# Weight sums issued by GpSimd in 45 marked steps of up to eight DMAs

## The chip, the cores and the metric

The kernel runs on one core of a Trainium2 chip. A core has TensorE (PE, matrix products), VectorE (DVE, elementwise), ScalarE (ACT, functions and copies), GpSimd (POOL) and SyncE (SP). SP, ACT and GpSimd also issue DMAs; each of the three has a queue of its own, and all share 16 DMA engines. The metric is the time of one execution on the device in microseconds. Three runs of the kernel before took 2488.29, 2488.68 and 2490.72 us.

## The reference

One decoder layer over 2048 tokens of width 1024, in float32, and a final norm:

```python
h = rmsnorm(x, mix_norm_g[l])
q, k, v, g, u = jnp.split(h @ w_in[l], [R, 2*R, 3*R, 4*R], axis=-1)      # R = 512
y_ret  = silu(g) * head_rmsnorm(retention(q, k, v, positions), ret_gn_g[l])   # 4 heads
y_pool = pool_mixer(u, pool_w[l], pool_scale[l])       # trailing means 2/4/8/16
x = x + jnp.concatenate([y_ret, y_pool], axis=-1) @ w_out[l]
x = x + cross_attn(rmsnorm(x, xa_norm_g[l]), mem_n, xa_wq[l], xa_wkv[l], xa_wo[l])   # 256 memory tokens
x = x + conv_glu_ffn(rmsnorm(x, ffn_norm_g[l]), ...)   # 2 x 2816 columns, causal conv of width 3
...
return rmsnorm(x, final_norm_g)
```

## The kernel before

Everything is kept transposed: a tile has 128 channels on the partitions and 512 tokens along the free side. Each float32 product is made from three matmuls in the reduced format fp32r (lines 266 to 268, the helper `passes`): high part by high part, high by low, low by high. A helper `split` (L258, ScalarE's copy, and L242, DVE's subtraction) makes the two parts.

The tokens go in two blocks of 1024 (`b` = 0 and 1). Block 0 passes through values, four retention heads, the pooling groups, the output projection (`add_residual`, whose x-tiles `fetch_x` loads at L556), the attention, and a projection with the folded value weights VWd. The attention multiplies with a folded score matrix Md: `load_m` (L905) fetches it in eight loads of 512 KB through the raw buffers R and S, and ScalarE splits each before its buffer is loaded again. At its first tile the attention also needs the norm of the tokens: squares on ScalarE (L387), sums on DVE (L242), and tiny matmuls (`stats`, L347) that add over the channels. Between the last tiles of block 0's attention DVE builds the rotary tables for block 1, which begins with a load of the positions (L585). During the VWd projection the tokens of block 1 are loaded and squared. Then block 1 runs: `values`, with `quarter_sums` (loads at L1524, ScalarE at L1532) beside it and the norm of the block (`stats`, a reciprocal root on DVE, and matmuls at L371 that spread it), then `head_projections`, output projection, attention and VWd projection. The feed-forward part of both blocks follows (`run`), from about 1225 us to the end.

In block 1's heads and in the whole feed-forward part a product of two by two blocks is made with seven block products instead of eight. That needs sums of blocks of the weights. They are made in DRAM by DMA: `weight_sums` (L975 to L994) is a generator over 42 jobs (8 of the input weights into Ad, 22 of w_up into Ud, 12 of w_dn into Dd). A job writes four blocks of 128 x 512 numbers (256 KB; 192 KB for four of the jobs) in five steps: SP copies two blocks (L986); GpSimd adds to both by accumulating DMAs (L988, L989); then twice a copy from a finished block (L992) and an addition to it (L994). Members of the feed-forward part and of block 1's heads load the finished sums later (L1070), through seven buffers of half a raw tile in block 1's heads.

The generator hangs in `under[0]`. The code that builds the matmuls takes one turn of it, `next(under[0], None)`, every so often: every second group of 12 matmuls in block 0's heads and pooling groups (`slow`), every group in the output projections, three turns per tile in block 0's attention and two in block 1's (`4 - pace`), one per call of `between` in block 1's values, one per product in block 1's heads. In the VWd projections it is set aside (`paused`). A turn places instructions in the program text only. The order on each engine is then chosen by a planner that simulates the kernel: instructions go by program order where they are ready, and later ones may run ahead. A job's copies on SP are bound only to come after the latest fetch on SP (`tc.issue_after(fetched[0].ins)`, order on that queue alone); GpSimd's DMAs wait for their data, and for nothing else. GpSimd has no other work in this part.

Of the kernel before, what the change touches and what calls it, by code (L numbers as in the profile page):

```python
# [11 lines left out]
AF = mybir.ActivationFunctionType  # L12
ALU = mybir.AluOpType
AX = mybir.AxisListType

P = 128
# [120 lines left out]
def trunk(ctx, tc, xT, memT, pos, w_qkgu, w_v, wkv, wqT, wo, wout_r, wout_p, poolT, w_up, w_dn, vecs, consts, outT):  # L137
# [162 lines left out]
        return X[:, 2 * k, s * SUB : (s + 1) * SUB], X[:, 2 * k + 1, s * SUB : (s + 1) * SUB]  # L300


    quarter, slow = [0], [True]
    behind, under, fetched = [iter(())], [iter(())], [None]
    turned, chained = [], []
    latest = [None]
# [585 lines left out]
    def attention(sums, beside, pace):  # L892
# [39 lines left out]
        for i in range(2 * KT):  # L932
# [20 lines left out]
            if len(late) == 2:  # L953
                turn(*late.pop(0))
            late.append((prob[hp], t, e))
            for _ in range(4 - pace):
                next(under[0], None)
            if i < KT - 2:
                next(more_m, None)
# [15 lines left out]
    def weight_sums():  # L975

        jobs = [((w_qkgu[a], w_qkgu[c]), 0, 4, Ad[p]) for p, (a, c) in enumerate(PAIRS)]
        jobs += [((w_up[f], w_up[f + NF]), 0, 4, Ud[f]) for f in range(NF)]
        for at, (k0, n) in enumerate(ROUNDS):
            jobs += [((w_dn[2 * j], w_dn[2 * j + 1]), k0, n, Dd[at, j]) for j in range(KT // 2)]  # L980
        for w, k0, n, to, in jobs:
            a11, a12, a21, a22 = (block(w, i // 2, i % 2, k0, n) for i in range(4))
            d = [to[i][:, : n * P] for i in range(4)]
            with tc.issue_after(fetched[0].ins):
                for i, a in ((2, a21), (0, a11)):
                    sp.dma_start(d[i], a)  # L986
            yield
            pool.dma_start(d[2], a22, accum_op=ALU.add, max_dma_last_dim=2048)  # L988
            pool.dma_start(d[0], a21, accum_op=ALU.add, max_dma_last_dim=2048)  # L989
            for at, was, a in ((1, 2, a11), (3, 1, a12)):  # L990
                yield
                pool.dma_start(d[at], d[was], max_dma_last_dim=2048)  # L992
                yield
                pool.dma_start(d[at], a, accum_op=ALU.add, max_dma_last_dim=2048)  # L994

    class Round:

# [861 lines left out]
    for b in range(NB):  # L1859
# [37 lines left out]
            mix = head_projections(b, v, rb, tabs, t1, t2, z3, z4)  # L1897
        for r in rb:
            r.free()
        slow[0] = False  # L1900

        xs = [TT.take() for _ in range(NS)]
        ahead = fetch_x(b, 0)
# [32 lines left out]
        def tables():  # L1936
            for got in rope_tables(b + 1):
                yield
            for i, r in enumerate(got):
                sp.dma_start(rope_d[i], r.f[:, :SUB])  # L1940
                r.free()

        beside = tables() if b + 1 < NB else first_tiles(own)
        prob, behind[0] = attention(xs, beside, b + 1)
        for _ in beside:
            pass
        under, paused = [iter(())], under
# [194 lines left out]
```

## Time and profile before

| What | us |
|---|---|
| median of three runs | 2488.68 |
| the profiled execution | 2485.41 |
| its span, first to last instruction | 2483.6 |
| PE busy | 2421.9 |
| DVE busy | 1728.7 |
| ACT busy | 1285.2 |
| POOL busy | 254.7 |

A wait in the profile is the idle time of an engine before an instruction, put down to what released it last. A DMA row gives the instruction's tiles (written <- read), the queue, the count, the size and the median time from issue to landing. In windows, the times are counted from the start of the span; the granted clock is 1.00 when TensorE runs at full speed.

### The profile page before, as it was taken

To read this page: it belongs to the slowest core of one execution; us is meant where nothing else is said; L and a number is where in the kernel's file an instruction comes from. 1 tells how busy PE (TensorE), PEld (TensorE's weight loads), DVE (VectorE), ACT (ScalarE), POOL (GpSimd) and SP (SyncE) were. 2 spreads that over 40 slices of the span, in tenths; PEclk is the share of its full clock that TensorE was granted. 3 is DMA by queue.
4 is the path that set the end of the run, shared out by engine and by line. 5 is a ranking of instruction groups with operands and counts; after the bars stand their busy time and mean duration, and the time that the engine had idled before them with its cause. 6 is when DMAs were issued, how large, how long until landed. Compare 5 with 4: busy or idle time off the path is not lost.

```text
span 2483.6 us, 33188 instructions
## 1 busy us (share of the span) xinstructions
PE 2421.9 (98%) x11294; PEld 2018.5 (81%) x11294; DVE 1728.7 (70%) x2921; ACT 1285.2 (52%) x2303; POOL 254.7 (10%) x356
## 2 busy tenths in 40 slices
PE   6999999899999999999999999999999999999997
PEld 6888888777777787888888888888888888888886
DVE  8646566555676666575688776897667688867875
ACT  6333423334444453434555555675555677666763
POOL 1110101352102222000000000020000000000000
PEclk9999999999999999999999999999999999999998
DMA  8463847998738779557458655665446468758951
GB/s 310 100 162 119 230 106 218 303 263 245 216 115 195 168 180 269 172 178 255 153 186 278 212 187 168 210 222 170 161 158 216 132 225 302 245 189 281 345 167 68
DMA packets 269820, 501.56 MB, mean 202 GB/s; under 512 B 28881, under 2 KB 58705, under 8 KB 269649
## 3 DMA queue, kind: packets, MB, share of 16 engines
q1 hardware_dynamic: 214352, 406.61, 49.0%
q0 software_dynamic: 30784, 64.50, 13.2%
q10 hardware_dynamic: 24512, 28.32, 3.3%
q8 instruction: 89, 1.46, 0.2%
q14 instruction: 83, 0.67, 0.1%
HBM read 398.13 MB, written 187.17 MB: 236 GB/s over the span
## 4 chain that ended last, share of the span: by engine, by line
PE 86%; DMA 6%; DVE 4%; ACT 2%; issue 1%; SPq 0%; POOLq 0%; POOL 0%; DVEq 0%; ACTq 0%
PE mm L266 27%; PE mm L268 27%; PE mm L267 27%; DMA T<-xT 2%; DMA Ud<-w_up 1%; DVE T L242 1%; DMA T<-pos 1%; DMA T<-Xd 1%; DVE Z L242 1%; PE aux L266 1%; PE aux L771 1%; PE aux L782 1%; PE aux L267 1%; PE aux L798 1%; PE aux L268 1%
## 5 line engine op out<-in xcount | busy, mean ns | idle before, releaser
L266 PE MATMUL mm<-G,Q 128*128 128x512 f32 (+1 forms) x1745 | 672.4, 386 | 22.1 <-ACT Q L258 11.7
L268 PE MATMUL mm<-G,Q 128*128 128x512 f32 (+1 forms) x1745 | 669.1, 384 | 5.9 <-DVE Q L242 5.7
L267 PE MATMUL mm<-G,Q 128*128 128x512 f32 (+1 forms) x1617 | 619.5, 383 | 0.0
L267 PE MATMUL mm<-G,E 128*128 128x512 f32 x1084 | 421.6, 389 | 0.0
L266 PE MATMUL mm<-G,E 128*128 128x512 f32 x1084 | 420.0, 389 | 0.0
L268 PE MATMUL mm<-G,E 128*128 128x512 f32 x1084 | 419.2, 389 | 0.0
L266 PEld LDWEIGHTS mm<-G,Q 128*128 128x128 f32 x1745 | 331.0, 190 | 88.8 <-ACT Q L258 13.3
L268 PEld LDWEIGHTS mm<-G,Q 128*128 128x128 f32 x1745 | 330.3, 189 | 71.4 <-DVE Q L242 8.7
L267 PEld LDWEIGHTS mm<-G,Q 128*128 128x128 f32 x1617 | 306.8, 190 | 56.2
L242 DVE TENSOR_TENSOR Z<-Z,mm 128x512 f32<-128x512 f32 x296 | 201.3, 681 | 98.5 <-PE mm L268 98.3
L250 DVE SCALAR_TENSOR_TENSOR Z<-Z,vecs 128x1024 f32<-128x1024 f32 x176 | 224.5, 1279 | 50.0 <-ACT Z L1139 46.4
L268 PEld LDWEIGHTS mm<-G,E 128*128 128x128 f32 x1084 | 203.5, 188 | 42.3
L266 PEld LDWEIGHTS mm<-G,E 128*128 128x128 f32 x1084 | 203.5, 188 | 42.1
L267 PEld LDWEIGHTS mm<-G,E 128*128 128x128 f32 x1084 | 203.5, 188 | 42.1
L1076 ACT ACTIVATE E<-R 128x512 fp32r<-128x512 f32 (+1 forms) x165 | 101.4, 615 | 140.8 <-PE mm L267 133.7
L242 DVE TENSOR_TENSOR T<-T 128x512 f32<-128x512 f32 (+3 forms) x217 | 148.4, 688 | 36.3 <-ACT T L387 20.7
L242 DVE TENSOR_TENSOR G<-T,G 128x512 fp32r<-128x512 f32 (+1 forms) x185 | 122.0, 674 | 41.4 <-ACT G L1025 30.4
L242 DVE TENSOR_TENSOR Q<-R,Q 128x512 fp32r<-128x512 f32 x149 | 103.4, 697 | 63.1 <-ACT Q L258 44.1
L1076 ACT ACTIVATE Q<-R 128x512 fp32r<-128x512 f32 (+1 forms) x153 | 94.5, 618 | 88.3 <-PE mm L267 75.8
L1025 ACT ACTIVATE G<-T 128x512 fp32r<-128x512 f32 x160 | 97.6, 624 | 57.9 <-DMA T<-Gd 27.7
L1139 ACT ACTIVATE Z<-Z,vecs 128x1024 f32<-128x1024 f32 x88 | 109.1, 1241 | 33.6 <-DVE Z L242 32.6
L242 DVE TENSOR_TENSOR E<-R,E 128x512 fp32r<-128x512 f32 (+1 forms) x131 | 87.4, 671 | 48.6 <-ACT E L1076 41.3
(323 smaller groups left out, 3674.5 us busy)
## 6 DMA issues: line engine op xcount, KB each, us to landing
T<-Gd SPq DMA_DIRECT2D x173, 256.0 KB, 4.4
Gd<-Z SPq DMA_DIRECT2D x110, 256.0 KB, 2.7
R<-Ud SPq DMA_DIRECT2D x106, 256.0 KB, 2.7
Ud<-w_up POOLq DMA_DIRECT2D x88, 256.0 KB, 8.6
R<-w_up SPq DMA_DIRECT2D x80, 256.0 KB, 2.9
S<-Ud SPq DMA_DIRECT2D x70, 256.0 KB, 2.8
T<-xT SPq DMA_DIRECT2D x64, 256.0 KB, 6.1
Gd<-T SPq DMA_DIRECT2D x56, 256.0 KB, 3.3
```

What stands on the lines that cost most here:

```text
L242: return eng.tensor_tensor(out=out, in0=a, in1=b, op=op)
L250: dve.scalar_tensor_tensor(out=out, in0=a, scalar=s, in1=b, op0=op0, op1=op1)
L266: pe.matmul(ps, lh, rh, start=start, stop=False, skip_group_check=more)
L267: pe.matmul(ps, lh, rl, start=False, stop=False, skip_group_check=more)
L268: latest[0] = pe.matmul(ps, ll, rh, start=False, stop=stop, skip_group_check=more)
L771: pe.matmul(col(sc, c), self.ch(k, c), self.ch(q, c), start=True, stop=True)
L782: pe.matmul(col(self.kv, c), col(self.kn.f, c), self.ch(v, c, h * T), start=True, stop=True)
L798: pe.matmul(col(y, c), col(self.pr.f, c), self.ch(v, c, h * T), start=True, stop=self.cur[c] is None)
L1025: act.activation(hi, x, AF.Copy)
L1076: act.activation(p2[:, 0, :w], self.raw[i].f[:, :w], AF.Copy)
L1139: act.activation(self.c[g].f, a[:, 2:], AF.Identity, bias=cb[:, f : f + 1], scale=cw[2][:, f : f + 1])
```

## The change

`weight_sums` becomes a loop over steps. Each job is itself a generator of four parts: four copies; two additions; one addition; one addition. GpSimd issues all eight. The second and fourth block no longer start from a copy of a finished sum but from a copy of a weight block, to which the finished sum is then added. In every step a new job is begun, and all begun jobs advance by one part, so from the fourth step on four jobs are under way and a step issues eight DMAs; 42 jobs make 45 steps. Ahead of each step ScalarE copies two columns into a place of `halo` (the mark), kept in program order behind what was traced before it on ScalarE; GpSimd copies the mark into another place of `halo`, and the step's DMAs are queued behind that copy. After a step, the generator passes `spacing[0]` turns: 4, but 8 in block 0's output projection and 2 in both attentions. The attention of block 0 now gives one turn per tile from the sixth tile on, and that of block 1 one per tile.

```diff
-    quarter, slow = [0], [True]
+    quarter, slow, spacing = [0], [True], [4]
...
-            for _ in range(4 - pace):
+            if pace > 1 or i > 4:
                 next(under[0], None)
...
-        for w, k0, n, to, in jobs:
+
+        def sums(w, k0, n, to):
             a11, a12, a21, a22 = (block(w, i // 2, i % 2, k0, n) for i in range(4))
             d = [to[i][:, : n * P] for i in range(4)]
-            with tc.issue_after(fetched[0].ins):
-                for i, a in ((2, a21), (0, a11)):
-                    sp.dma_start(d[i], a)
-            yield
-            pool.dma_start(d[2], a22, accum_op=ALU.add, max_dma_last_dim=2048)
-            pool.dma_start(d[0], a21, accum_op=ALU.add, max_dma_last_dim=2048)
-            for at, was, a in ((1, 2, a11), (3, 1, a12)):
+
+            def add(at, a):
+                pool.dma_start(d[at], a, accum_op=ALU.add, max_dma_last_dim=2048)
+
+            for i, a in ((2, a21), (0, a11), (1, a11), (3, a12)):
+                pool.dma_start(d[i], a, max_dma_last_dim=2048)
+            yield
+            add(2, a22)
+            add(0, a21)
+            yield
+            add(1, d[2])
+            yield
+            add(3, d[1])
+
+        live, jobs, at = [], [sums(*j) for j in jobs], 0
+        while jobs or live:
+            if jobs:
+                live.append(jobs.pop(0))
+            at += 1
+            here, there = halo[:, at % 32], halo[:, 40]
+            tc.keep_in_program_order(act.activation(here, cs_t[:, P : P + 2], AF.Copy))
+            turn = pool.tensor_copy(there, here)
+            with tc.issue_after(turn.ins):
+                live = [g for g in live if next(g, True) is None]
+            for _ in range(spacing[0]):
                 yield
-                pool.dma_start(d[at], d[was], max_dma_last_dim=2048)
-                yield
-                pool.dma_start(d[at], a, accum_op=ALU.add, max_dma_last_dim=2048)
...
-        slow[0] = False
+        slow[0], spacing[0] = False, (8, 4)[b]
...
+        spacing[0] = (2, 2)[b]
         prob, behind[0] = attention(xs, beside, b + 1)
+        spacing[0] = 4
```

## The prediction

> **What bounds the kernel now.** I read the page's busy shares first, then the stages that overlap the weight sums, then TensorE's waits in them, and last the DMAs by stage.
>
> ```profile
> span 2483.6 us, 33188 instructions
> PE 2421.9 (98%) x11294; PEld 2018.5 (81%) x11294; DVE 1728.7 (70%) x2921; ACT 1285.2 (52%) x2303; POOL 254.7 (10%) x356
> ```
>
> TensorE is the bound: 2421.9 of 2483.6 us, so at most 61.7 us of idle time (plus what a lowered clock costs) can be won at all. The weight sums run beside the stages of the next fence and end with them. In it (the windows view) the columns are stretch, length, then busy time and instructions of each engine, granted clock, DMA share, GB/s.
>
> ```profile
> 62.00:399.00 337.00, 337.00 (x1791) 290.27 (x1791) 209.84 (x451) 121.95 (x262) 29.44 (x41) 1.00 0.52 142
> 399.00:486.00 87.00, 78.65 (x349) 64.35 (x348) 43.80 (x69) 32.00 (x55) 27.64 (x38) 0.97 1.05 294
> 486.00:576.00 90.00, 85.91 (x393) 70.37 (x394) 52.12 (x133) 37.15 (x87) 41.92 (x57) 0.97 1.07 264
> 576.00:690.00 114.00, 111.72 (x509) 91.33 (x508) 62.46 (x111) 45.40 (x81) 13.21 (x18) 1.00 0.74 224
> 690.00:738.00 48.00, 46.40 (x195) 38.15 (x196) 34.51 (x70) 21.03 (x35) 1.64 (x2) 0.94 0.32 96
> 738.00:941.00 203.00, 197.19 (x1018) 164.69 (x1016) 135.16 (x277) 99.40 (x234) 46.82 (x64) 1.00 0.73 178
> 941.00:1026.00 85.00, 82.48 (x357) 67.03 (x356) 53.16 (x87) 35.41 (x62) 21.94 (x30) 0.98 1.01 293
> ```
>
> These are the heads, output projection and attention of the first block of tokens (b = 0), the folded value projection, then values, heads and output projection of the second (b = 1). Idle time of PE is length less busy: 0, 8.35, 4.09, 2.28, 1.60, 5.81, 2.52, together 24.65 us. The two worst stages are the two whose DMA share is over 1.
>
> ```profile
> PE aux L347 <- DVE T L242: 6.8, 1, 6.8
> PE aux L920 <- DVE T L246: 4.1, 3, 1.8
> PE mm L266 <- ACT Q L1076: 3.0, 4, 1.3
> PE aux L371 <- DVE Q L242: 2.8, 1, 2.8
> ```
>
> That is the head of PE's waits from 434 to 992 us (total, times, longest). One single wait of 6.8 us stands out. The timeline of PE around it:
>
> ```profile
> 485.61 1.87 PE L347 MATMUL aux<-consts,T 128*128 128x1 f32 x8 [6.82 <-DVE T L242]
> 487.92 0.63 PE L268 MATMUL mm<-G 128*128 128x512 f32 x1
> 490.90 0.63 PE L266 MATMUL mm<-G 128*128 128x512 f32 x1
> 491.83 0.39 PE L266 MATMUL mm<-G 128*128 128x512 f32 x1
> ```
>
> After the idle time the matmuls take 0.63 us instead of 0.39, eight of them from 487.92 to 490.90: 8 x 0.24 = 1.9 us more. So this place at the start of b = 0's attention costs 8.35 + 1.9, about 10 us. What is late there:
>
> ```profile
> DVE T L246 <- DMA T<-pos: 9.1, 1, 9.1
> ACT T L387 <- DMA R<-Md: 6.5, 1, 6.5
> ```
>
> (waits from 480 to 535 us.) ScalarE stands at a square (L387) behind splits of the score matrix Md, whose load had not landed; DVE's sum and then PE's L347 wait for that square. The DMAs issued from 399 to 486 us (count, size, median us to landing):
>
> ```profile
> Ud<-w_up POOLq DMA_DIRECT2D x22, 256.0 KB, 8.6
> Ud<-w_up SPq DMA_DIRECT2D x19, 256.0 KB, 12.5
> Ud<-Ud POOLq DMA_DIRECT2D x11, 256.0 KB, 7.1
> R<-Md SPq DMA_DIRECT2D x5, 512.0 KB, 12.4
> ```
>
> Weight sums are 52 of them in these rows, 19 in SP's own queue, between the loads that PE needs. That is the wait the change bears on.
>
> **The change, part by part.** *Work.* Each of the 42 jobs moved 8 DMAs before (2 copies on SP; 4 additions and 2 copies on GpSimd) and moves 8 after (4 copies, 4 additions, all on GpSimd): 336 either way, the same bytes to within the source of two copies. Nothing is saved in transfer; only when and on which queue.
>
> *When.* Before, a job takes 5 steps of the generator; SP's copies are only queued behind the latest fetch and GpSimd's only wait for data, so both run ahead of the program. After, step n issues at a place fixed by ScalarE's mark. By the loops: the heads of b = 0 give 32 turns, spacing 4, so 8 steps; its output projection 32 turns, spacing 8, 4 steps; its attention 11 turns, spacing 2, 6 steps; the values of b = 1 16 turns, 4 steps; its heads 56 turns, 14 steps; its output projection 32 turns, 8 steps; one step is left for its attention. That is 45. Steps issue 4, 6, 7, then 8 each, the last three 4, 2, 1. By stage: 57, 32, 48, 0 (folded value projection), 32, 112, 54, 1.
>
> *First output projection (399 to 486).* 52 or more sums become 32, in four bursts 21 us apart (87/4), and none of them in the ring in which Md's loads stand. Bounds: 0 (a burst covers Md's loads and they land as late as now) to -10. Nearest row for Md with fewer sums about is the last stage's, quoted below: 7.4 instead of 12.4 us. The loads form a chain (a buffer is loaded again once ScalarE has split it), so 5 us less on each of the last three is more than the 6.8 us wait. I take -9.
>
> *First attention (486 to 576).* The positions are loaded early in it, before its first burst (its turns begin with the sixth tile); DVE's 9.1 us wait for them goes, and with it the one L920 wait of 1.8 that follows. Bounds 0 to -1.8; I take -1.5. The other L920 waits follow ScalarE's exponentials and stay.
>
> *Folded value projection (576 to 690) and values (690 to 738).* The sums leave the first and enter the second. The row of x-loads in two parts of the first, 600 to 645 beside sums and 652 to 692 without:
>
> ```profile
> T<-xT SPq DMA_DIRECT2D x8, 256.0 KB, 7.0
> Ud<-w_up POOLq DMA_DIRECT2D x12, 256.0 KB, 9.0
> Ud<-w_up SPq DMA_DIRECT2D x6, 256.0 KB, 5.6
> ...
> T<-xT SPq DMA_DIRECT2D x15, 256.0 KB, 4.2
> ```
>
> Faster x-loads at 600 hide behind PE, which idles 2.28 us in that stage for other reasons: 0. But the mark of the first step of the values follows a ScalarE instruction of the stage before, and ScalarE is idle there, waiting:
>
> ```profile
> ACT T L1532 <- DMA T<-xT: 5.9, 1, 5.9
> DVE T L242 <- ACT T L1532: 4.5, 1, 4.5
> ```
>
> (waits from 676 to 692.) So the burst can issue at about 680, just when the x-loads of the quarter sums are issued; DVE stands behind those with the reciprocal root that PE's L371 awaits. A load of 4.2 then takes about 7.0: +2.8 on a wait of 2.8. Bounds: -5 (wait and its slow clock, some 2 us, gone because the order falls otherwise) to +5 (the load delayed by 2.8, and the slow clock once more). I take +2.5.
>
> *Heads of b = 1 (738 to 941).* 112 sums, where 5 turns a job gave 56/5 = 11 jobs, 90 DMAs. ScalarE waits for a DMA once in the stage:
>
> ```profile
> ACT S L1076 <- DMA R<-Ad: 3.1, 1, 3.1
> ```
>
> The loads are fetched up to seven ahead, one per 2.7 us of matmuls (12 x 0.23), so 7 us instead of 4 is covered; if that cover is gone, each late load shows at PE. Bounds -1 to +4; I take 0.
>
> *Second output projection (941 to 1026).* 54 sums, against:
>
> ```profile
> Dd<-w_dn POOLq DMA_DIRECT2D x20, 256.0 KB, 7.9
> T<-xT SPq DMA_DIRECT2D x14, 256.0 KB, 9.6
> Dd<-Dd POOLq DMA_DIRECT2D x10, 256.0 KB, 6.5
> S<-Md SPq DMA_DIRECT2D x4, 512.0 KB, 7.4
> Dd<-w_dn SPq DMA_DIRECT2D x7, 256.0 KB, 7.9
> ```
>
> 37 become 54 where the DMA share is 1.01 already. This is the density of the bad stage (52), though the last 7 DMAs come thin. Bounds 0 to +11 (the price of the first attention's start, 10, and one for the residual loads). I take +1.
>
> *Issue and marks.* Row by row, nanoseconds min/median/max:
>
> ```profile
> L986 SPq DMA_DIRECT2D Ud<-w_up x44: 490/512/1096, 398.9 to 779.2; - x44
> L992 POOL DMA_DIRECT2D Ud<-Ud x44: 523/554/832, 413.8 to 798.8; - x44
> L994 POOL DMA_DIRECT2D Ud<-w_up x44: 800/834/1732, 422.1 to 802.8; - x44
> L804 ACT ACTIVATE T<-aux x32: 268/277/288, 791.0 to 928.0; 128x128 f32<-128x128 f32 x32
> ```
>
> SP loses 84 issues of 0.51 us, 43 us spread over 940; it lets later loads out sooner, counted above. A step costs GpSimd 4 x 0.55 + 4 x 0.83 = 5.5 us, under the shortest distance of steps (two tiles of 24 matmuls x 0.23, 11 us); GpSimd is 10% busy and no one waits for it here, so 0. Its additions wait inside the queue for the step before; behind them stand only later sums. The mark is smaller than L804's tile: 45 x at most 0.28 = 13 us on an engine 52% busy, with PE behind it in few places: 0 to +1, I take 0. Were ScalarE's slack gone, all 13 us would show.
>
> **Sum.** -9 - 1.5 + 2.5 + 0 + 1 = -7 us. The profiled execution took 2485.41 (span 2483.6 and 1.8 around it), so 2478.4 on its scale; the median of the runs is 3.27 above it, and 2488.7 - 7 = 2481.7 is what I forecast.
>
> A rule that bears on the first term: the Trainium skill, "DMA: Bandwidth & Descriptors", section "Issuing engines are not separate DMA queues", says that all queues end on the same 16 DMA engines and that issuing from another engine saves only the sequencer's time; by it the 84 moved copies bring no landing time, only the thinning counts, and the first term would be half, the sum about -2.5. The same page, section "Queues, rings and completion order", says that each engine goes round its queues packet by packet; by that a load no longer stands behind copies of its own ring, and the sum stays at -7. No row here separates the two, since sums stood in both queues throughout.
>
> **Rivals.**
> 1. *The stall moves to the start of b = 1's attention.* With 54 sums the second output projection has the first one's density, Md's loads go from 7.4 towards 12.4 us, and ScalarE's splits hold up the square as they do at 485. Against it: the last three steps thin out before the end, and no PE wait of this kind is there now. It decides if Md's last loads land after about 1026. Price 10, with +5 at the values: -9 - 1.5 + 5 + 1 + 10 = +5.5, 2494.
> 2. *Landing follows the bytes in flight, not the queue.* A burst is 8 x 256 KB at once where GpSimd now has one job's few DMAs in flight; a burst at about 464 (the fourth in that stage) covers Md's last loads. For it: x-loads take 7.0 beside sums two thirds of which are GpSimd's. Half of the first term is lost: -9 + 4.5 - 1.5 + 2.5 + 1 = -2.5, 2486. The page's first rule above is this one.
> 3. *All stalls that hang on the sums' traffic go*, L371's too: -10 - 1.8 - 5 = -17, 2472. For it: the order on each engine is a planner's, and would be drawn anew; against: DVE's stand between 676 and 692 has no sums beside it.
>
> **How the numbers follow.** About 5 us (0.2%) is what a measurement of this kernel can tell from no change. My case has 0.45 (of it 0.36 beyond -5 and 0.09 within); rival 1 0.27, slower; rival 2 0.13, within; rival 3 0.15, faster. So faster 0.51, same 0.22, slower 0.27. The predicted time is 2481.7. The range runs from just inside rival 3 (2471) to just past rival 1 (2496); my case alone spans -4 to -10, 2478 to 2485.
>
> **What would show it.** The wait of L347 at about 480 gone or under 2 us, with no matmuls of 0.63 after it; R<-Md from 399 to 486 at 6 to 9 us; no wait of DVE for pos over 4 us; T<-xT issued near 680 at 6 us or more and L371's wait between 2 and 6 us; no sums issued by SP and none from 590 to 675; PE's idle time from 941 to 1040 under 4 us. Wrong it would be if the second output projection or the second attention's start shows a PE wait over 5 us, if marks on ScalarE wait for GpSimd, or if the planner's new order opens waits away from the sums.

## The result, and the profile after

The changed kernel took 2489.68 us (median of 12 runs, 2487.23 to 2494.33) against 2487.89 for the kernel before (12 runs beside them): a ratio of 1.0014, with a 95% interval of 1.0004 to 1.0025. So it is slower by 0.14%, less than the 0.2% set as the bound, and 8 us above the forecast of 2481.7. The profiled execution took 2488.75 us, 3.3 more than the one before.

The page of the changed kernel, for the two page lines shown of before:

```profile
span 2487.0 us, 33308 instructions
PE 2424.5 (97%) x11294; PEld 2021.6 (81%) x11294; DVE 1731.5 (70%) x2921; ACT 1288.9 (52%) x2348; POOL 319.2 (13%) x485
```

PE's idle time is 62.5 us now and was 61.7. That sum hides a great deal, as the stages show. In the windows view of the changed kernel (columns as before), cut at the same matmuls of the program as the stages of before, the rows are: heads, output projection and attention of b = 0; then, behind the folded value projection (left out, no idle time), values, heads, output projection and attention of b = 1.

```profile
62.00:403.80 341.80, 339.43 (x1808) 292.44 (x1808) 211.24 (x452) 123.57 (x274) 48.60 (x77) 1.00 0.54 150
403.80:481.60 77.80, 77.80 (x349) 64.53 (x348) 45.21 (x71) 32.90 (x59) 17.00 (x26) 1.00 0.87 250
481.60:564.20 82.60, 82.60 (x393) 68.30 (x392) 51.14 (x132) 36.67 (x90) 29.20 (x45) 1.00 0.63 148
...
674.60:729.50 54.90, 47.68 (x196) 38.26 (x197) 34.26 (x64) 21.89 (x41) 25.10 (x36) 0.94 0.87 218
729.50:939.80 210.30, 200.20 (x1017) 166.47 (x1016) 138.24 (x283) 101.44 (x249) 77.81 (x120) 0.98 0.75 191
939.80:1022.90 83.10, 81.06 (x357) 66.06 (x357) 50.14 (x82) 33.47 (x63) 34.66 (x55) 1.00 1.07 317
1022.90:1119.60 96.70, 92.93 (x431) 76.49 (x432) 61.51 (x146) 31.75 (x85) 4.23 (x6) 0.96 0.56 167
```

The output projection and the attention of b = 0 have no idle time left (8.35 and 4.09 us before), and the clock is full in both. The values and the heads of b = 1 have it instead: 7.22 us (1.60 before) and 10.10 (5.81). The second output projection idles as before (2.04 us, 2.52 before); the second attention, which ran without a gap before, has 3.77, and the heads of b = 0, also without a gap before, 2.37.

```profile
1026.00:1116.00 90.00, 90.00 (x432) 74.61 (x432) 60.26 (x144) 29.43 (x80) 0.00 (x0) 1.00 0.39 134
```

(That row is the kernel before, the same attention.) The waits of PE in the changed kernel from 60 to 1130 us:

```profile
PE mm L266 <- ACT Q L1092: 6.0, 4, 4.3
PE mm L266 <- ACT E L1659: 4.7, 1, 4.7
PE aux L920 <- DVE T L246: 4.7, 2, 3.8
PE aux L371 <- DVE Q L242: 2.6, 1, 2.6
...
PE mm L266 <- ACT T L504: 2.4, 1, 2.4
```

L347's 6.8 us are gone. New are 4.7 us at 721 (L1659), 4.3 at 748 (L1092), 3.8 at 1038 (L920) and 2.4 at 221 (L504). (Lines behind 975 lie 16 further down than before: L1092 was L1076.)

How the two kernels drift apart can be worked out from the traces. PE runs 11,294 matmuls in both, so the start of the n-th in one trace less the start of the n-th in the other says how far one is behind (plus) or ahead at that piece of work. In us against before:

```
n       before at  changed   what lies since the row above
400         76.7     +2.0    start of the program
2400       473.5     +4.7    heads b = 0 (the wait at 221), output projection
2800       574.0    -11.8    start of the attention, attention b = 0
3400       712.3    -16.5    folded value projection, values b = 1
3600       759.3     -2.1    end of the values, first products of the heads
4800      1007.5     -3.3    heads, output projection b = 1
5000      1049.7     +3.5    start of the second attention
11000     2402.5     +3.6    feed-forward part
```

So the change did win its 16.5 us at the place it bears on. It lost 14.4 within 47 us of work around the end of the values and 6.8 at the second attention. Each loss is more than the waits shown, since the clock is halved after them (granted clock 0.50 from 721.6 to 726.7, from 749.1 to 753.8 and from 1040.8 to 1044.2 us); the timeline of PE behind the wait at 1038:

```profile
1038.59 2.03 PE L920 MATMUL aux<-consts,T 128*128 128x128 f32 x8 [3.77 <-DVE T L246]
...
1040.85 0.63 PE L267 MATMUL mm<-Q,G 128*128 128x512 f32 x1
1041.28 0.63 PE L268 MATMUL mm<-Q,G 128*128 128x512 f32 x1
```

These start 0.43 us apart for some 3.5 us, where a matmul takes 0.23 otherwise.

The chain behind the loss at 721, in the waits from 695 to 722:

```profile
ACT G L1562 <- DVE T L250: 10.1, 1, 10.1
DVE Z L250 <- DMA T<-xT: 9.7, 2, 8.3
...
PE mm L266 <- ACT E L1659: 4.7, 1, 4.7
```

The second row is the first in time: DVE waits 8.3 us for one x-load of the quarter sums, which is issued at 704.0 and lands 8.3 us later (the same load of before took 2.6); ScalarE stands at L1562 (`negated`, which copies a quarter sum) 10.1 us for DVE; behind it on ScalarE, in order, stands L1659, which empties a bank of products, and PE waits for that bank. Before, DVE's longest wait for x here was 1.8 us. The DMAs issued from 680 to 720 in the changed kernel:

```profile
Ud<-w_up POOLq DMA_DIRECT2D x18, 256.0 KB, 10.0
T<-xT SPq DMA_DIRECT2D x8, 256.0 KB, 5.2
```

The 18 DMAs from w_up (12 copies and 6 additions; further additions read finished sums) are new in this stretch; before had no sums in it, and its x-loads landed in 3.6. The median hides how far the x-loads go apart: 3.4 to 12.3 us. The wait at 748 is simpler. ScalarE has to split a raw tile of Ad for the next product, and the load, issued at 739.4, is not there until 745.3:

```profile
745.37 0.63 ACT L1092 ACTIVATE S<-R 128x512 fp32r<-128x512 f32 x1 [4.74 <-DMA R<-Ad]
```

PE waits 4.3 us right behind it. The wait at 1038 comes from Md, in the waits from 1005 to 1040:

```profile
DVE Z L242 <- ACT Z L258: 11.7, 3, 5.3
...
ACT Z L258 <- DMA S<-Md: 7.5, 2, 5.5
ACT Z L258 <- DMA R<-Md: 7.2, 2, 5.4
...
PE aux L920 <- DVE T L246: 3.8, 1, 3.8
```

ScalarE's splits of Md wait for the loads, DVE's halves of the splits for ScalarE, and PE stands at L920 behind DVE. The last of these loads lands at 1029.6; DVE has the first small step of the norm, whose sums PE's L347 makes from 1022 to 1024, in order behind the halves of that split, so it comes to it at 1031.5. Md is late beside what is issued with it (938 to 1022):

```profile
Dd<-w_dn POOLq DMA_DIRECT2D x38, 256.0 KB, 13.2
...
Dd<-Dd POOLq DMA_DIRECT2D x11, 256.0 KB, 13.9
S<-Md SPq DMA_DIRECT2D x4, 512.0 KB, 10.6
R<-Md SPq DMA_DIRECT2D x4, 512.0 KB, 13.8
```

49 sums where there were 37, and Md's loads land in 10.6 to 13.8 us (7.4 before for S<-Md, 7.2 for R<-Md). In the first output projection it went the other way (405 to 478): 21 sums of Ud in GpSimd's queue in three bursts (12 copies, 9 additions), and

```profile
R<-Md SPq DMA_DIRECT2D x5, 512.0 KB, 5.5
...
S<-Md SPq DMA_DIRECT2D x3, 512.0 KB, 6.4
```

against 12.4 and 13.0 before.

### The profile page after: what moved, and what is told of

It is laid out like the page before. It is cut to its first block, busy times and chain, and to the rows that moved or that the text cites. A ratio compares the mean times of both kernels' runs of the same rounds, so it can differ in the third digit from the quotient of the medians.

```text
span 2487.0 us, 33308 instructions
## 1 busy us (share of the span) xinstructions
PE 2424.5 (97%) x11294; PEld 2021.6 (81%) x11294; DVE 1731.5 (70%) x2921; ACT 1288.9 (52%) x2348; POOL 319.2 (13%) x485
## 4 chain that ended last, share of the span: by engine, by line
PE 89%; DMA 4%; DVE 4%; ACT 2%; issue 1%; SPq 0%; POOLq 0%; POOL 0%; DVEq 0%; ACTq 0%
PE mm L266 28%; PE mm L267 28%; PE mm L268 28%; DMA T<-xT 1%; DVE T L242 1%; DMA T<-Xd 1%; PE aux L266 1%; PE aux L782 1%; PE aux L267 1%; PE aux L268 1%; PE aux L798 1%; PE aux L771 1%; DMA R<-Md 1%; PE aux L800 1%; DVE Z L242 0%
## 5 line engine op out<-in xcount | busy, mean ns | idle before, releaser
L266 PEld LDWEIGHTS mm<-G,Q 128*128 128x128 f32 x1745 | 332.8, 191 | 96.1 <-ACT Q L258 12.1
L242 DVE TENSOR_TENSOR Z<-Z,mm 128x512 f32<-128x512 f32 x296 | 202.1, 684 | 104.7 <-PE mm L268 104.4
L242 DVE TENSOR_TENSOR T<-T 128x512 f32<-128x512 f32 (+3 forms) x217 | 148.9, 689 | 39.5 <-ACT T L387 15.6
L1092 ACT ACTIVATE E<-R 128x512 fp32r<-128x512 f32 (+1 forms) x165 | 101.5, 615 | 143.0 <-PE mm L267 132.6
L242 DVE TENSOR_TENSOR G<-T,G 128x512 fp32r<-128x512 f32 (+1 forms) x185 | 122.6, 676 | 41.8 <-ACT G L1041 31.4
L242 DVE TENSOR_TENSOR Q<-R,Q 128x512 fp32r<-128x512 f32 x149 | 103.6, 698 | 65.1 <-ACT Q L258 46.0
L1092 ACT ACTIVATE Q<-R 128x512 fp32r<-128x512 f32 (+1 forms) x153 | 94.4, 617 | 88.0 <-PE mm L267 77.3
L1092 ACT ACTIVATE E<-S 128x512 fp32r<-128x512 f32 (+1 forms) x107 | 65.8, 616 | 105.7 <-PE mm L267 104.4
```

The lines of the kernel that those rows point to most:

```text
L242: return eng.tensor_tensor(out=out, in0=a, in1=b, op=op)
L266: pe.matmul(ps, lh, rh, start=start, stop=False, skip_group_check=more)
L1092: act.activation(p2[:, 0, :w], self.raw[i].f[:, :w], AF.Copy)
```

## The experiments

The theory they start from: the win at the first attention comes from fewer sums beside Md's loads, and each loss from sums that now stand beside loads with little slack, that is, loads that an engine stands waiting for soon after their issue. Rivals: the win comes from the queue (sums left SP's ring); the losses come from the size of the bursts, from the marks on ScalarE, or from the planner's new order.

**1. No turns in the values of b = 1.** The sums return to a stretch that begins only with the heads.

```diff
-                if next(more_sums, None) is None:
-                    next(under[0], None)
+                next(more_sums, None)
```

> The changed kernel, but the values of the second block give no turns to the weight sums; its four steps there move on, and the last of them into the second attention. If the sums beside the x-loads of the quarter sums cause the two new waits of PE (5.1 us at 721, 4.6 at 749, with their slow clock 14 us against before between matmuls 3200 and 3600 of the program), those 14 us go and the run takes 2476 to 2480, up to 5 more if the second attention is then disturbed more. If the planner's new order of instructions causes them, they stay and the run takes 2487 to 2492.

Measured: 2474.61 us, ratio to before 0.9958 (0.9946 to 0.9971), by the ratios some 14 us less than the change as it was made. DVE's wait for x in 690 to 722 is 2.1 us instead of 9.7, and the PE wait at 721 is gone. What is left, from 60 to 1250 us:

```profile
PE mm L266 <- ACT Q L1092: 5.2, 4, 3.5
PE aux L920 <- DVE T L246: 4.6, 5, 1.5
```

PE is 20.8 us ahead at n = 3400 and still 17.0 at 3600; 4.8 are lost from n = 4800 to 6000 around the second attention. So the loss around the end of the values comes with the sums there: 3.8 us are lost from n = 3400 to 3600 instead of 14.4. The wait of 3.5 us for Ad at 735 stays, which experiment 5 takes up. The loss at the start of the second attention shrank too (1.7 us from n = 4800 to 5000 instead of 6.8), although 61 sums, more than the change's 48, stand in the output projection ahead of it and Md lands in 8.9 to 14.8 us there. The last load of Md lands as late, measured by PE's work (1016.0 us, with PE 13.4 us further), but DVE has the norm's first small step ahead of the halves of that split, at 1011.7, and not behind them. So the late load opens that loss, and as far as the traces tell the order on DVE, which the planner drew, sets most of its size.

**2. Spacing 4 in the first output projection as well.** All sums stay in GpSimd's queue; only their density goes back up.

```diff
-        slow[0], spacing[0] = False, (8, 4)[b]
+        slow[0], spacing[0] = False, 4
```

> The changed kernel with a spacing of 4 in the first output projection too: eight steps (64 sums) there instead of four (32), and only five at the head of the second output projection. If thinning cured the start of the first attention, its wait comes back (10 to 16 us more between matmuls 2400 and 2800) and the wait of 4.2 us at 1039 goes (7 less): 2493 to 2499. If the change of queue and the marks cured it, it stays cured and only the 7 us go: 2482 to 2484.

Measured: 2494.01 us, 1.0037 (1.0022 to 1.0053). The old stall is back at 487.6 us, a little longer than before (7.4 us). The head of PE's waits, then the DMAs from 410 to 490:

```profile
PE aux L347 <- DVE T L242: 7.4, 1, 7.4
```

```profile
Ud<-w_up POOLq DMA_DIRECT2D x31, 256.0 KB, 12.4
...
Ud<-Ud POOLq DMA_DIRECT2D x10, 256.0 KB, 11.4
R<-Md SPq DMA_DIRECT2D x5, 512.0 KB, 12.1
...
S<-Md SPq DMA_DIRECT2D x3, 512.0 KB, 15.5
```

No sum is in SP's queue, and Md lands in 12.1 to 15.5 us as it did with 19 of them there (12.4). So what cures that stall is the thinning, not the other queue. 5.1 of the 16.5 us from n = 2400 to 2800 stay won here; nearly all of them lie in the attention behind the stall, and no run tells which part of the change won them. The jobs done earlier here are missing at the end: the wait at 1038 is gone, and in the windows of 955 to 1036 us Md lands in 5.4 to 6.8. The same traffic moved from one place to the other, and the stall went with it.

**3. The queue alone.** The kernel before, with SP's copies given to GpSimd.

```diff
-            with tc.issue_after(fetched[0].ins):
-                for i, a in ((2, a21), (0, a11)):
-                    sp.dma_start(d[i], a)
+            for i, a in ((2, a21), (0, a11)):
+                pool.dma_start(d[i], a, max_dma_last_dim=2048)
```

> The kernel before, with the two copies of each job issued by GpSimd instead of SP, and nothing else changed: no marks, no interleaving, the same turns. If Md's loads were late because they stood behind copies in SP's own ring, most of the 6.8 us wait at 486 goes and the run is 5 to 10 us faster than before. If landing follows the bytes in flight, the wait stays within 2 us and the run stays within 4 us of before.

Measured: 2583.47 us, 1.0391 (1.0372 to 1.041), which none of the theories foresaw. The edit also took away the tie to the latest fetch. GpSimd then issued all 336 sums from the start of the program, done by 452 us; the page's slices show it (GpSimd and the DMA engines):

```profile
POOL 4454455000000000000000100011000010000000
...
DMA  9999999343243222437656856475546568857951
```

PE's longest wait is 34.7 us, until 69.8 us, and it is for GpSimd's own arithmetic: at the start of the program GpSimd also makes sums for a norm (L242), and the last of them, which starts at 15.7 us in the kernel before, starts at 68.7 here, since it stands in order among DMAs that wait for data. PE is 122.8 us behind by n = 2400. As a test of the queue it fails, because it changed the time of the sums as well; experiment 2 answers that question. It does show that sums which no one ties down do not stay where the program text has them.

**4. The marks alone.** The kernel before, with one ScalarE copy in program order and one GpSimd copy for each job.

```diff
-        for w, k0, n, to, in jobs:
+        for job, (w, k0, n, to) in enumerate(jobs):
+            tc.keep_in_program_order(act.activation(halo[:, job % 32], cs_t[:, P : P + 2], AF.Copy))
+            pool.tensor_copy(halo[:, 40], halo[:, job % 32])
```

> The kernel before, with a mark of ScalarE and its copy by GpSimd at the beginning of each of the 42 jobs, which nothing is queued behind on purpose. My term for the marks was 0 to 1 us: 2487 to 2490. If marks hold ScalarE up (each waiting for GpSimd, or moving the planner's order), the run is more than 3 us away from before, and the trace shows ScalarE or PE waiting at marks.

Measured: 2487.44 us, 1.0004 (0.9992 to 1.0016). A mark costs ScalarE 0.19 us:

```profile
L982 ACT ACTIVATE halo<-consts x42: 185/188/252, 77.8 to 981.0; 128x2 f32<-128x2 f32 x42
```

42 of them are 8 us of ScalarE, and by the interval at most half of it shows.

**5. No turns in the values, none in the first product group of the heads.** Aimed at the wait for Ad at 735 that experiment 1 left.

```diff
+            if m is not members[0]:
                 next(under[0], None)
...
-                if next(more_sums, None) is None:
-                    next(under[0], None)
+                next(more_sums, None)
```

> e1 without turns in the seven products of the first member of the second block's heads either. If the wait that is left in e1 at 735 (3.5 us behind ScalarE's L1092, which waits 5.3 us for a load of Ad that took 6.4) comes from the burst beside that load, it falls back to the 1.3 us that the kernel before has there, 3 to 4 us with the slow clock. Two steps more go to the second attention, for 0 to 4 us. 2469 to 2476. If that wait is the planner's and not the burst's, it stays, and the run is at 2474 to 2479.

Measured: 2478.7 us, 0.9978 (0.9968 to 0.9989). The wait at 735 is gone: ScalarE waits 1.5 us for Ad there, PE 0.5, and PE is 18.1 us ahead at n = 3600. Three later loads of Ad, issued from 739.8 to 751.2, took 7.0 to 7.4 us, and PE waited for none of them over 1 us: by then the loads have a lead. But jobs were pushed to the end. At n = 5000 it is 11.7 ahead, at 6000 only 5.7, with L347 now late at the second attention by 3.1 us and a loss of 6.0 us from 1083 to 1110, in the last part of that attention, which has 39 sums. By the ratios that is 5 us worse than experiment 1.

**6. The same with spacing 3 in the heads of b = 0.** More sums early, so that fewer are left for the end; the marks behind fall at other places too.

```diff
-    quarter, slow, spacing = [0], [True], [4]
+    quarter, slow, spacing = [0], [True], [3]
```

> e5 with a spacing of 3 instead of 4 in the first block's heads, so that about eleven steps instead of eight are made there and the second attention gets three fewer. If DMA traffic is free in the heads, nothing is lost there but the wait of 2.3 us at 221, and the second attention's waits between 1097 and 1108 (about 3 us) go: 2466 to 2472. If bursts delay the loads of the folded weights, the wait at 221 grows or new ones open before 400, 3 to 8 us: 2472 to 2480.

Measured: 2477.43 us, 0.9976 (0.9962 to 0.999). The end is hardly better (8.3 ahead at n = 6000), and the wait for Ad is back, because a mark now falls at 724 us and its burst meets the load issued at 728. Waits from 724 to 740 here:

```profile
ACT S L1092 <- DMA R<-Ad: 5.9, 1, 5.9
...
PE mm L266 <- ACT Q L1092: 4.1, 1, 4.1
```

That one load took 7.0 us; in experiment 5, whose first mark is at 735, it took 2.7. Beside experiment 5 this settles the wait for Ad: it is one load without slack, late when a burst stands beside it.

**7. Half bursts at the same density.** Each step in two halves with a mark each, at half the distance.

```diff
+            for half in range(2):
...
+                    if half == 0:
+                        live = [g for g in live if next(g, True) is None]
+                    elif jobs:
+                        live.append(sums(*jobs.pop(0)))
+                        next(live[-1])
+                for _ in range(spacing[0] // 2):
+                    yield
```

> The changed kernel with each step cut in two, each half behind a mark of its own and after half the turns: the additions first, the new job's four copies after. The density of the sums is the same, a burst has four DMAs. If it is the eight DMAs in flight at once that hold up the loads (the x-loads at 700, the loads of Ad at 740, Md at 1000, the folded weights at 210), the new waits shrink by half or more, 8 to 12 us less: 2477 to 2482. If it is the density, the waits stay and the run is within 3 us of the changed kernel, 2487 to 2492.

Measured: 2489.6 us, 1.0013 (0.9998 to 1.0029), the change's own time. The waits at 721 and 1038 stand in it, the first of them longer:

```profile
PE mm L266 <- ACT E L1662: 6.8, 1, 6.8
PE aux L920 <- DVE T L246: 5.6, 2, 3.8
```

The first is the one at 721, the second's 3.8 the one at 1038. The wait for Ad is 2.8 us instead of 4.3, and one of 3.8 at 955 is new. But the bursts were halved only in part. In block 0's output projection GpSimd issues four at a time, 11 us apart. At the places that lose, the marks of two halves fall together on ScalarE (672.0 and 672.0, 687.8 and 687.8, 957.4 and 957.5), and GpSimd issues eight sums from 670 to 675, seven from 694 to 701 and eight from 716 to 720. In the second output projection GpSimd issues sums almost without a break in both kernels. So this run does not show whether the size of a burst or the number of sums makes those loads late.

**8. Experiment 5 with a thin end.** Spacing 8 in both output projections, no turns in the second attention, and the generator not set aside in block 1's VWd projection (spacing 3 there).

```diff
-            if pace > 1 or i > 4:
+            if pace == 1 and i > 4:
...
-        slow[0], spacing[0] = False, (8, 4)[b]
+        slow[0], spacing[0] = False, 8
...
-        spacing[0] = 4
+        spacing[0] = (4, 3)[b]
...
-        under, paused = [iter(())], under
+        paused = under
+        if b + 1 < NB:
+            under = [iter(())]
```

> e5 with the second block's output projection at a spacing of 8 (four steps, 32 sums, as in the first block), no turns in the second attention, and the remaining eleven steps or so in the second block's projection with VWd, at a spacing of 3. If the waits at 1012 (3.1 us, L347) and from 1082 to 1108 in e5 come from the sums beside Md and beside the second attention's tiles, all 12 us that e5 loses after matmul 4600 go, less 0 to 6 for sums beside the loads of T from Hd at 1120 to 1220: 2467 to 2475. If those waits belong to the order of the planner, they stay: 2476 to 2482.

Measured: 2479.44 us, 0.9969 (0.9959 to 0.9978). The second attention is clean now (21.3 us ahead at n = 3600, 20.5 at 4800 and 5000), and 13.5 us are lost right behind it, where the rest of the sums went, 71 of them; the longest wait there is 4.6 us, at 1224. The loss was moved, not cured.

**9. Experiment 1 with that end, but spacing 4 in the second output projection.**

```diff
-            if pace > 1 or i > 4:
+            if pace == 1 and i > 4:
...
-                if next(more_sums, None) is None:
-                    next(under[0], None)
+                next(more_sums, None)
...
-        spacing[0] = 4
+        spacing[0] = (4, 3)[b]
...
-        under, paused = [iter(())], under
+        paused = under
+        if b + 1 < NB:
+            under = [iter(())]
```

> e1 with no turns in the second attention; its output projection before that stays at a spacing of 4 (64 sums), and the last five steps go to the projection with VWd. The waits from 1097 to 1108 go (3 us less than e1), the start of the second attention stays as in e1, where Md took 9 to 15 us: 2470 to 2475. If the density in the output projection is what costs at the attention's start, matmuls 4800 to 5000 show 2 to 7 us here and nothing in e8.

Measured: 2477.77 us, 0.9963 (0.9949 to 0.9978). As experiment 1 within what the runs tell: the wait for Ad at 735 is there (3.4 us), 1.5 us are lost at the second attention, and 6.5 behind it.

**10. The heads of b = 0 twice as dense.** Spacing 2 there, 5 in the second output projection, no turns in the values, and none in the first ten products of block 1's heads.

```diff
-    quarter, slow, spacing = [0], [True], [4]
+    quarter, slow, spacing = [0], [True], [2]
...
+            if at >= 10:
                 next(under[0], None)
...
-        slow[0], spacing[0] = False, (8, 4)[b]
+        slow[0], spacing[0] = False, (8, 5)[b]
```

> The changed kernel with the sums moved to where the runs so far show DMA traffic to cost least: a spacing of 2 in the first block's heads (16 steps), none in the second block's values and in the first ten products of its heads, a spacing of 5 in its output projection, and only the last one or two steps, of one to four DMAs, in its attention. If the waits follow the sums beside loads without slack, matmuls 3400 to 5200 lose nothing against e5's best, the total there is about 20 us ahead of the kernel before, and the only cost is the first block's heads, 0 to 8 us: 2466 to 2474. If the heads have no room for 113 sums, waits on the folded weights open between 130 and 400 and the run is at 2475 to 2485.

Measured: 2485.55 us, 1.0001 (0.999 to 1.0012). Three new stalls in the heads of b = 0, the first behind loads of the attention's output weights (ScalarE waits 8.8 us for `S<-wo` there):

```profile
PE mm L266 <- ACT T L504: 7.7, 1, 7.7
PE mm L266 <- ACT T L522: 6.6, 2, 6.4
PE aux L782 <- ACT T L777: 2.8, 1, 2.8
```

PE is 25.9 us behind by n = 2400. From there to the end nothing goes wrong, and it finishes 1.3 ahead: the later part is 27 us faster than before. The 2.4 us wait at 221 in the changed kernel stands at the same line, behind a load of the same weights (ScalarE waits 3.5 us for `S<-wo`).

**11. The rest of the sums in the feed-forward part.** Spacing 4 in the heads as in the change, the omissions of experiment 10, and what is left over is neither pressed into the second attention nor issued at its end, but taken one step per 14 items of the feed-forward loop (marks in another tile there).

```diff
-            if pace > 1 or i > 4:
+            if pace == 1 and i > 4:
...
+            if at % 14 == 13:
+                next(under[0], None)
...
+            if at >= 10:
                 next(under[0], None)
...
-                if next(more_sums, None) is None:
-                    next(under[0], None)
+                next(more_sums, None)
...
-        slow[0], spacing[0] = False, (8, 4)[b]
+        slow[0], spacing[0] = False, (8, 5)[b]
...
-        spacing[0] = (2, 2)[b]
+        spacing[0] = (2, 1)[b]
...
-        spacing[0] = 4
+        spacing[0] = (4, 1)[b]
...
-    for _ in under[0]:
-        pass
```

> The changed kernel with no sums in the second block's values, in the first ten products of its heads and in its attention, a spacing of 5 in its output projection, and the last nine steps or so (sums of w_dn only, marks in another small tile) in the feed-forward part of the first block, one every 14 products, 38 us apart. If every wait so far follows sums beside loads without slack, matmuls 3400 to 5200 lose nothing, the lead there is about 20 us, and the feed-forward part, where a step comes every 38 us, costs 0 to 5: 2465 to 2472. If a step beside the feed-forward part's loads opens waits there as it did in the projection before it in e8 (13 us), the run is at 2474 to 2480.

Measured: 2468.1 us (6 runs, 2465.07 to 2470.43), ratio to before 0.9931 (0.9916 to 0.9946): by the ratios about 17 us less than before and 20 less than the change as it was made, and the best of all that was run. Its windows for the values, heads, output projection and attention of b = 1, cut at the same matmuls:

```profile
673.80:718.20 44.40, 44.40 (x197) 36.63 (x196) 32.69 (x63) 19.77 (x34) 0.00 (x0) 1.00 0.28 78
718.20:919.70 201.50, 196.93 (x1018) 164.74 (x1016) 135.57 (x278) 101.26 (x248) 81.02 (x126) 1.00 0.84 212
919.70:1004.10 84.40, 82.38 (x357) 67.29 (x357) 52.53 (x86) 35.29 (x65) 24.41 (x38) 0.98 0.94 272
1004.10:1094.10 90.00, 90.00 (x430) 74.61 (x431) 59.55 (x144) 29.41 (x80) 0.00 (x0) 1.00 0.40 134
```

The DMA share went from 0.87 to 0.28 in the values and from 1.07 to 0.94 in the output projection. PE's idle time went from 7.22 us to nothing in the values, from 10.10 to 4.57 in the heads and from 3.77 to nothing in the attention; the output projection's 2.02 us were there in the changed kernel (2.04) and before. The last mark falls at 1562 us; the 55 sums in the feed-forward part come with a loss of 2.6 us (n = 6000 to 11000 below).

The drift of the changed kernel and of the experiments built on it, side by side (us against before, as in the table above; the number is the experiment's):

```
n       changed     1      2      5      6      7      8      9     10     11
400       +2.0   +0.7   +0.6   +2.3   +1.2   +2.1   +1.0   +1.3   +1.7   +2.0
2400      +4.7   +3.2   +3.1   +6.6   +5.9   +4.0   +3.4   +3.3  +25.9   +4.0
2800     -11.8  -13.3   -2.0   -9.9  -10.1  -12.5  -13.1  -13.2   +9.5  -12.5
3400     -16.5  -20.8   -7.8  -17.4  -17.6  -20.0  -20.6  -20.7   +2.0  -20.0
3600      -2.1  -17.0   +9.0  -18.1  -13.2   -5.8  -21.3  -17.0   +1.2  -20.7
4800      -3.3  -16.7   +9.3  -17.9  -16.1   -3.4  -20.5  -16.7   -1.4  -22.0
5000      +3.5  -15.0   +9.3  -11.7  -11.2   +3.5  -20.5  -15.2   -1.4  -22.0
6000      +3.6  -11.9   +9.4   -5.7   -8.3   +4.5   -7.0   -8.7   -1.2  -21.1
11000     +3.6  -11.5   +9.4   -5.7   -8.3   +5.5   -7.0   -8.7   -1.3  -18.5
```

Each column is one profiled execution, so a difference of a microsecond or two in it is not evidence.

## Why the prediction was wrong

*First output projection, -9, and first attention, -1.5: right in the mechanism, too small.* The L347 wait and the slow matmuls are gone, Md lands in 5.5 to 6.4 us (6 to 9 was said), and DVE's wait for the positions fell from 9.1 to 4.4 (I had said not over 4). From n = 2400 to 2800 PE won 16.5 us where 10.5 were in the sum. The 4.09 us that PE idled in the attention went altogether, and I had given it 1.5. With the 8.35 of the output projection that is 12.4 us of idle time; most of the rest is the slow clock, which I had at 1.9. The stage also got fewer sums than I had counted, 22 and not 32 (55 before). That the thinning cures the stall, not the queue, is experiment 2. The rule that I set against the first term (the Trainium skill, "DMA: Bandwidth & Descriptors", section "Issuing engines are not separate DMA queues"), that issuing from another engine saves only the sequencer's time, agrees with that run: with no sum in SP's queue Md still took 12.1 to 15.5 us. My step from it, that half of the term would then be lost, was wrong: the stall came back whole with the density (7.4 us against 6.8).

*Folded value projection and values, +2.5: this is the step that failed.* I saw that a burst could issue at 680 beside the x-loads of the quarter sums, and priced the one wait that was already there, L371's at 690. That wait did not grow (2.6 us against 2.8), and the slow clock behind it went, so that with the other work around it 4.7 us were won from n = 2800 to 3400. The burst did issue at 678.5, and four x-loads issued beside it (679.2 to 680.7) took 5.2 to 12.3 us; but L371's wait was over at 680.4, before any of them landed. The price lay with a later x-load: I had the whole stage's sums (32) in the text, and looked only at the first burst of them. DVE's longest wait for x went from 1.8 us to 8.3, for a load issued at 704.0 between the bursts of 697 and 705, and two engines downstream PE stood 4.7 us at 721, plus the slow clock.

*Heads of b = 1, 0 (bounds -1 to +4): failed too.* "Fetched up to seven ahead, so 7 us instead of 4 is covered" holds for the middle of the stage and not for its beginning, where no lead has been built up. The load that ScalarE waited 4.7 us for is such a one, and the trace of before had hinted at it: its single ScalarE wait for Ad, 3.1 us, was quoted beside the sentence that called the loads covered. Experiments 5 and 6 show it: 2.7 us or 7.0 us for the same load, by whether a burst stands beside it, while loads of 7 us from 740 us on cost PE no more than 1 us. The two steps together were +2.5 and measured +14.4 from n = 3400 to 3600, of which some 11 are undone by taking out the turns in the values (experiment 1, -20.8 to -17.0 there).

*Second output projection, +1: too small.* 6.8 us were lost from n = 4800 to 5000, and PE's idle time from 941 to 1040 us is 5.8 (under 4 was to show my case). Rival 1 had the mechanism and the place: the sums as dense as in the bad stage, Md's loads late (10.6 to 13.8 us) and the stall at the start of b = 1's attention. It was off in the line, L920 and not L347, and in the price: 3.8 us of wait and the slow clock, not 10. Its total of 2494 took 5 for the values where 14.4 came, and -10.5 for the first output projection and attention where -16.5 came; the slower result is thus rival 1 in its sign and its second half only. The number of sums alone does not give the price: with 21 to 32 sums in that output projection nothing is lost from n = 4800 to 5000 (experiments 2, 8, 10, 11), with 48 to 57 it is 4.9 to 6.9 us (the change, 5, 6, 7), but with 61 and 59 only 1.7 and 1.5 (1 and 9). The late load was there in all six; in the four with the large loss DVE has the norm's first small step behind the halves of Md's last split, in experiments 1 and 9 ahead of them.

*Issue and marks, 0: right for the marks* (experiment 4), which did not wait for GpSimd on ScalarE. The count of steps by stage was not: 67, 22, 40, 16, 32, 106, 48 and 5 sums by the trace, where I had 57, 32, 48, 0, 32, 112, 54 and 1. ScalarE reaches some marks a stage early, so that eight sums went out from 655.7 to 659.5, though I had said none from 590 to 675. And a step is not always issued at its mark. I had a step at 5.5 us of GpSimd, under the distance of the marks; but GpSimd also waits in order for earlier sums to land, 38 us in all from 938 to 1022 us, and comes to the marks of the second output projection 4 to 26 us late. There the marks no longer set where the sums stand.

*Rival 2, bytes in flight in bursts:* it was wrong for the first term, which was won in full. For the losses it is not settled, since experiment 7 did not halve the bursts where they lie. What the runs do show is that it depends on whether sums stand beside loads that have no slack.

*Rival 3, all stalls that hang on the sums' traffic go,* is not what the change does, but it is what it could do: 16.5 to 20.8 us ahead by n = 3400 in all but two of the kernels that keep its loop (2 and 10, where stages ahead of it were made denser).

*Not in the sum at all:* 2.0 us by n = 400, where no sum has been issued, and 2.7 from there to n = 2400, where the wait at 221 (2.4 us, behind the loads of the output weights) is new. For that stage I had costed nothing, since PE never idled in it; from 62 to 400 us 65 sums are issued where 56 were, in bursts of eight, and ScalarE waits 3.5 us for a load of the output weights in front of that place. Twice the density there cost 24.2 us (experiment 10, n = 400 to 2400). The 2.0 us at the start vary between 0.6 and 2.3 over the kernels that keep the change's loop; what causes them was not tried.

The sum as measured is +2.0 +2.7 -16.5 -4.7 +14.4 -1.2 +6.8 +0.1 = +3.6 by n = 11000, against +3.3 between the profiled executions and +1.8 between the medians.

What stays open: why the second attention loses another 3 to 6 us behind its start in experiments 1, 5 and 6; which of the leftover sums does it was not separated. No run held the planner's order fixed while the sums moved, so its share is read from the traces alone. Nor was experiment 11 taken apart; it changes four things that the other runs had shown one by one or two by two.

## What to carry to other kernels

A transfer that is moved off a bad place must be priced at every place it goes to, and there by the loads with the least slack: the first loads after a change of stage, and those behind which another engine stands in order. A wait that an engine off the bound already shows for such a load, as ScalarE's 3.1 us for Ad before, marks a place to look at before more traffic is put there, even though PE hardly waits there. A stage's DMA share alone does not tell where work that nothing needs soon can go. The heads of b = 0 had a share of 0.52 before, and 128 sums in them (experiment 10) cost 24.2 us; the last projection had 0.66, and 71 sums in its 109 us (experiment 8) cost 13.5; the feed-forward part had 0.62, and 55 sums in steps some 38 us apart (experiment 11) cost 2.6. Moving the sums off the loads without slack was worth 20 us over the change as it was made.

## What the runs showed of the hardware

The clock can be lost after short idle times. In the kernel before, around 945 us, three within 4 us came ahead of it (0.50, 0.55 and 1.27 us):

```profile
941.61 0.50 PE L266 MATMUL mm<-G,Q 128*128 128x512 f32 x1 [0.50 <-ACT Q L258]
...
943.36 0.50 PE L268 MATMUL mm<-G,Q 128*128 128x512 f32 x1 [0.55 <-DVE Q L242]
...
945.36 1.65 PE L266 MATMUL mm<-E,Q 128*128 128x512 f32 x3 [1.27 <-ACT E L258]
946.80 0.63 PE L267 MATMUL mm<-E,Q 128*128 128x512 f32 x1
```

Matmuls of 0.63 us follow until 948.5; the granted clock is 0.57 from 945 to 949 us and 1.00 in the 5 us ahead of that. The Trainium skill, "TensorE: Matmul & The Clock Gate", Part 1, speaks of an idle window of about 3.4 us; a single gap of that length is not needed here. Nor does the length of one gap decide it: the wait of 2.8 us at 691.6 in the kernel before is followed by ten matmuls at the slow rate, the one of 2.6 at 680.4 in the changed kernel by none. The waits of 3.8 to 4.7 us in the changed kernel are each followed by 9 to 13 matmuls that start 0.43 us apart instead of 0.23, which makes 2 to 3 us more (9 to 13 x 0.2): a sum of waits alone leaves out a third of each loss or more.

DMAs that GpSimd issues without a tie ran far ahead of the program text: in experiment 3, all 336 within the first 452 us, and the execution took 98 us longer (2583.47 against 2485.39 for the runs of before beside it). An engine's arithmetic stands in one order with the DMAs that it issues: GpSimd's last sum for the norm started 53 us later there (68.7 against 15.7).
